# Two Strassen–Winograd products moved to the pre-MLP norm, and the sums of the down weights moved into down

## The chip, the core and the metric

The kernel runs on one core of one Trainium2 chip. The engines that matter here are TensorE (PE, matrix products), VectorE (DVE) and ScalarE (ACT), which work element by element, GpSimd (POOL), and SyncE (SP), on whose queue every transfer of this part of the kernel is issued. Each engine takes its instructions strictly in order; an instruction that waits holds up everything behind it on that engine. The metric is the device time of one execution in microseconds (us), as the median of several runs.

## The reference

One layer of a hybrid decoder trunk, 1024 tokens by 1024 channels, all in float32: two mixers on a common projection, merged and projected, then an MLP with a squared ReLU.

```python
x = x + rms_norm(merged @ w_o, norm_mix_post)
h = rms_norm(x, norm_mlp_pre)
u = jnp.square(jax.nn.relu(h @ w_mlp_up))            # 1024 x 1024 by 1024 x 4096
x = x + rms_norm(u @ w_mlp_down, norm_mlp_post)      # 1024 x 4096 by 4096 x 1024
```

Only the stretch from the last norm on is touched; the mixers ahead of it stay as they are.

## The kernel before, in words

**Precision.** Every float32 operand is split into a high and a low part (h and l at the end of a name: ACT's CAST at L234 makes the high part, DVE's subtraction at L164 the low one), and `mm3` (L254) makes a product of three matmuls: high by high, high by low, low by high. The row of a program order shows the first two as "x2", since they use the same weights.

**Strassen–Winograd.** Both large products of the MLP are made by blocks, two by two, with seven products P1 to P7 in place of eight. In up, the blocks of h are R11, R21, R22 (P1, P2, P3) and four sums, T1 to T4 (P5, P6, P7, P4), called "big" in the trace. The blocks of the weights are made per unit.

**The norm (up to L1130).** Tokens are worked in two halves, u = 0 and 1. For each, PE multiplies by w_o, then four tiles of 128 tokens are normed one by one: x loaded, added, stored (d_x1), squared, scaled (the tile m), transposed by PE in two groups into the banks "t" and "l" (`mt` and `ml` in the trace), and copied and split into the blocks. After the first half R11 and R21 are complete; R22 and T1 to T4 need the second.

**Up (L1133 to L1263)** runs over 16 units n; unit n holds hidden columns 128n on and 2048 + 128n on. `prep(n)` loads the two halves of its weights (wu, 512 KB each) two units ahead, and DVE makes the weight sums P3, P5, P6, P7 of them (four operations). `product` splits one such block of weights (wh, wl: three buffers) and issues 12 matmuls, four steps of three. P1, P6, P7 and P4 add up in one accumulator bank A ("r" for even units, "o" for odd ones, so mr and mo in the trace); after each, the bank is copied out (c11, c12, c22, c21). P2 has a bank of its own, and P5 and P3 share another, C ("g"). The copies, with C added where it belongs, then Relu and Square, give the four blocks of u; `u_sums` (four DVE operations) makes the three sums and one difference that down needs. All seven are stored in d_u. The order by which PE takes a unit's products is written out by hand in the loop: P6, P5, P7, P1 of the next unit, P4, P2 of the next unit, P3.

`down_sums(j)`, in the same loop, loads one row block of the down weights (wd, two loads of 512 KB), makes their four Strassen sums on DVE and stores them (d_t, 1024 KB).

**Down (L1268 to L1366)** makes the seven products again, each over eight steps j; a step is `fetch` (ru from d_u, rv from the weights or from d_t, 512 KB each, four buffers each; both split) and 24 matmuls into four banks of 128 tokens by 512 columns. The order is P1, P2, P6, P5, P7, P4, P3.

**What sets the order.** The Tile framework gives each instruction a priority from its place in the code; `tc.high_priority` moves pieces ahead (HP = 2000 for splits and weight sums, HPM = 1500 for what frees a bank). All transfers go to SP's queue, in the order that comes of this. A tile of a new stage waits until the tile that held its memory before is no longer used.

Of the kernel before, what the change touches and what calls it, by code (L numbers as in the profile page):

```python
# [16 lines left out]
P = 128  # L17
# [114 lines left out]
def kernel(  # L132
# [925 lines left out]
    with tc.tile_pool(name="op", bufs=1, reuse_waits="tile") as op:  # L1058
# [10 lines left out]
        for u in range(2):  # L1069
# [19 lines left out]
            for i in range(4):  # L1089
                t = u * 4 + i  # L1090
                tsl = slice(t * P, t * P + P)
                rs = op.tile([P, 1], F32, tag="rs", name="rs", bufs=3)
                tt(rs, s2s[i][:, 0:1], s2s[i][:, 1:2], ALU.add, eng=G)
                rsqrt(rs, rs, 1.0 / D, EPS)
                m = ms[i]
                xt = op.tile([P, D], F32, tag="xt", name="xt", bufs=2)
                SP.dma_start(out=xt, in_=x2[tsl, :])
                stt(xt, m, rs, xt, ALU.mult, ALU.add)
                SP.dma_start(out=d_x1[tsl, :], in_=xt)
                rs = op.tile([P, 1], F32, tag="rs", name="rs", bufs=3)  # L1100
                act(m, xt, AF.Square, accum_out=rs)
                rsqrt(rs, rs, 1.0 / D, EPS)
                stt(m, xt, rs, wpre2, ALU.mult, ALU.mult)
                il = slice(i * P, i * P + P)
                pv = []
                for g in range(2):
                    pt = mbank("tl"[g])
                    for k in range(4):
                        T.transpose(out=pt[:, k * P:(k + 1) * P], in_=m[:, (g * 4 + k) * P:(g * 4 + k + 1) * P],
                                    identity=ident)  # L1110
                    pv.append(pt.rearrange("p (k c) -> p k c", c=P))
                if u == 0:
                    for g, n in enumerate(("11", "21")):
                        A.copy(out=X[n][:, :, il], in_=pv[g])
                        hilo(R[n], k4, il, X[n][:, :, il])
                else:
                    x11, x21, x12, x22 = (X[n][:, :, il] for n in ("11", "21", "12", "22"))
                    A.copy(out=x12, in_=pv[0])
                    tt(x22, pv[1], x12, ALU.subtract)
                    hilo(R["22"], k4, il, pv[1])  # L1120
                    tt(x12, x12, x11, ALU.subtract)
                    tt(x11, x22, x11, ALU.add)
                    hilo(T2, k4, il, x11)
                    hilo(T1, k4, il, x12)
# [9 lines left out]
    with tc.tile_pool(name="ml", bufs=1, reuse_waits="tile") as ml:  # L1134
# [20 lines left out]
                mm3(ps, hi[:, k, :], lo[:, k, :], RT[p][:, k, :], RT[p][:, 4 + k, :], first and k == 0, k == 3, not first)  # L1155

        def ev(nm):
            return ml.tile([P, 512], F32, tag="ev", name=nm, bufs=8)
# [5 lines left out]
        def store(b, n, t):  # L1164
            SP.dma_start(out=d_u[b, :, n, :], in_=t)


        def down_sums(j):
            w = ml.tile([P, 4, 512], F32, tag="wd", name="wd", bufs=2)
            for f in range(2):  # L1170
                SP.dma_start(out=w[:, 2 * f:2 * f + 2, :].rearrange("p c n -> p (c n)"), in_=wdn[:, j + NU * f, :])
            tt(w[:, 3], w[:, 3], w[:, 1], ALU.subtract)
            tt(w[:, 1], w[:, 1], w[:, 0], ALU.subtract)
            tt(w[:, 0], w[:, 3], w[:, 0], ALU.add)
            tt(w[:, 2], w[:, 2], w[:, 0], ALU.subtract)
            SP.dma_start(out=d_t[:, j], in_=w)

        def s_P1(n):
            x = un[n]
# [14 lines left out]

        def s_P6(n):
            x = un[n]
            product(n, "P6", x["A"], False)
            x["c12"] = ev("c12")
            with tc.high_priority(offset=HPM):
                A.copy(out=x["c12"], in_=x["A"])  # L1200

        def s_P5(n):
            x = un[n]
# [3 lines left out]
        def s_P7(n):  # L1207
            x = un[n]
            product(n, "P7", x["A"], False)
            x["c22"] = ev("c22")  # L1210
            with tc.high_priority(offset=HPM):
                A.copy(out=x["c22"], in_=x["A"])
                tt(x["c22"], x["C"], x["c22"], ALU.add)
            relu2(x["c22"], x["c22"])
            store(2, n, x["c22"])

        def s_P4(n):
# [1 line left out]
            product(n, "P4", x["A"], False)  # L1219
            x["c21"] = ev("c21")  # L1220
            with tc.high_priority(offset=HPM):
                act(x["c21"], x["A"], AF.Relu)
            act(x["c21"], x["c21"], AF.Square)
            store(1, n, x["c21"])

# [40 lines left out]


    with tc.tile_pool(name="dn", bufs=1, reuse_waits="tile") as dn:  # L1268
        wpost2 = dn.tile([P, D], F32, name="wpost2")
        SP.dma_start(out=wpost2, in_=norm_mlp_post[0].unsqueeze(0).broadcast_to([P, D]))  # L1270
        act(wpost2, wpost2, AF.Copy, scale=D ** 0.5)
        sums = dn.tile([P, P], F32, name="sums")[:, 0:3 * NTOK].rearrange("p (t c) -> p t c", c=3)

        def wd_raw(f, c):
            return lambda j: wdn[:, f * NU + j:f * NU + j + 2, c * 512:c * 512 + 512]

        def wd_sum(b):
            return lambda j: d_t[:, j:j + 2, b, :]

        LR = dict(P1=(0, wd_raw(0, 0)), P2=(1, wd_raw(1, 0)), P3=(6, wd_raw(1, 1)), P4=(2, wd_sum(2)),  # L1280
                  P5=(3, wd_sum(1)), P6=(4, wd_sum(0)), P7=(5, wd_sum(3)))

        def fetch(p, j):
            out = []
            for src, tag in ((d_u[LR[p][0], :, j:j + 2, :], "u"), (LR[p][1](j), "v")):
                raw = dn.tile([P, 2, 512], F32, tag="r" + tag, name="r" + tag, bufs=4)
                SP.dma_start(out=raw, in_=src)
                out.append(split(raw, [P, 2, 512], dn, tag, 3))
            return out

        def products(p, banks, first, tail=False):
            todo = []
# [104 lines left out]
```

## Time and profile before

| | before |
|---|---|
| median of 3 runs | 1748.56 us (1748.1 to 1748.99) |
| profiled execution | 1746.59 us |
| its span on the core | 1744.9 us |
| mean granted PE clock | 0.982 |
| PE busy | 1658.3 us (95%) |
| DVE / ACT / POOL busy | 980.7 / 781.5 / 130.7 us |
| HBM read / written | 173.21 / 70.28 MB |

The span is the core's own stretch from first to last instruction; the execution's time is 1.7 us longer. In a "windows" row the stretch and its length stand first, then the busy time of PE, of its weight loads, of DVE, ACT and POOL, each with the number of instructions, then the granted PE clock, the mean busy share of the 16 DMA engines, and GB/s. In a "timeline" row the start and the duration of an instruction stand first, and in brackets at its end the time for which its engine had been idle, and what it waited for. In a row on DMA issues the last figure is the median time from issue to landing.

### The profile page before, as it was taken

To read this page: it belongs to the slowest core of one execution; us is meant where nothing else is said; L and a number is where in the kernel's file an instruction comes from. 1 tells how busy PE (TensorE), PEld (TensorE's weight loads), DVE (VectorE), ACT (ScalarE), POOL (GpSimd) and SP (SyncE) were. 2 spreads that over 40 slices of the span, in tenths; PEclk is the share of its full clock that TensorE was granted. 3 is DMA by queue.
4 is the path that set the end of the run, shared out by engine and by line. 5 is a ranking of instruction groups with operands and counts; after the bars stand their busy time and mean duration, and the time that the engine had idled before them with its cause. 6 is when DMAs were issued, how large, how long until landed. Compare 5 with 4: busy or idle time off the path is not lost.

```text
span 1744.9 us, 24420 instructions
## 1 busy us (share of the span) xinstructions
PE 1658.3 (95%) x9174; PEld 1405.2 (81%) x9174; DVE 980.7 (56%) x1678; ACT 781.5 (45%) x1593; POOL 130.7 (7%) x221
## 2 busy tenths in 40 slices
PE   7999999999999999999999996799999969999997
PEld 6887778878899998998788874588888858888886
DVE  5677466752544436442453466787785544544554
ACT  5455545653433235433321353555555544443442
POOL 2010111111000000101000022000000000000021
PEclk9999999999999999999999997899999989999999
DMA  5222213222212121116543452689884367666663
GB/s 166 58 76 70 80 41 92 78 73 80 61 43 61 44 61 37 50 49 206 162 142 99 139 175 85 222 321 330 318 286 166 122 240 253 194 194 194 194 218 136
DMA packets 168613, 245.10 MB, mean 140 GB/s; under 512 B 21943, under 2 KB 98830, under 8 KB 166446
## 3 DMA queue, kind: packets, MB, share of 16 engines
q1 hardware_dynamic: 168494, 243.53, 42.9%
q8 instruction: 72, 1.18, 0.3%
q14 instruction: 47, 0.39, 0.1%
HBM read 173.21 MB, written 70.28 MB: 140 GB/s over the span
## 4 chain that ended last, share of the span: by engine, by line
PE 81%; DVE 7%; ACT 5%; DMA 4%; issue 2%; POOL 1%; SPq 0%; DVEq 0%; ACTq 0%; POOLq 0%
PE g L66 56%; PE mr L66 9%; PE mo L66 8%; PE ml L66 3%; PE mt L66 3%; DMA gb<-d_g 1%; DVE Xt L164 1%; PE mt L70 1%; DVE Xi L545 1%; DMA oraw<-d_ob 1%; DMA d_sig<-sg 1%; DVE X L164 1%; ACT E L176 1%; DVE wl L164 1%; ACT wh L234 0%
## 5 line engine op out<-in xcount | busy, mean ns | idle before, releaser
L164 DVE TENSOR_TENSOR wl<-w,wh 128x512 fp32r<-128x512 f32 x165 | 114.7, 696 | 224.6 <-ACT wh L234 223.2
L66 PE MATMUL g<-hT,wh 128*128 128x512 f32 (+1 forms) x600 | 239.0, 399 | 1.6 <-DVE gr L173 0.9
L66 PE MATMUL g<-hL,wh 128*128 128x512 f32 (+1 forms) x600 | 232.8, 388 | 0.0
L66 PE MATMUL g<-hT,wl 128*128 128x512 f32 (+1 forms) x600 | 232.0, 387 | 0.0
L234 ACT CAST wh<-w 128x512 fp32r<-128x512 f32 x168 | 104.0, 619 | 203.7 <-PE g L66 179.2
L66 PE MATMUL g<-wh,hT 128*128 128x256 f32 x640 | 185.6, 290 | 0.0
L66 PE MATMUL g<-wl,hT 128*128 128x256 f32 x640 | 182.1, 285 | 0.0
L66 PE MATMUL g<-wh,hL 128*128 128x256 f32 x640 | 182.0, 284 | 0.0
L164 DVE TENSOR_TENSOR ul<-ru,uh 128x1024 fp32r<-128x1024 f32 x56 | 68.6, 1224 | 152.5 <-ACT uh L234 152.2
L66 PEld LDWEIGHTS g<-hT,wh 128*128 128x128 f32 x600 | 113.4, 189 | 22.0 <-ACT sg L176 1.4
L66 PEld LDWEIGHTS g<-hT,wl 128*128 128x128 f32 x600 | 113.3, 189 | 21.5 <-DVE wl L164 0.2
L234 ACT CAST uh<-ru 128x1024 fp32r<-128x1024 f32 x56 | 58.9, 1052 | 159.1 <-PE g L66 92.2
L66 PEld LDWEIGHTS g<-hL,wh 128*128 128x128 f32 x600 | 113.6, 189 | 18.8 <-issue 1.0
L66 PEld LDWEIGHTS g<-wh,hT 128*128 128x128 f32 x640 | 123.1, 192 | 1.4 <-issue 1.0
L66 PEld LDWEIGHTS g<-wl,hT 128*128 128x128 f32 x640 | 123.2, 192 | 1.2 <-issue 1.0
L66 PEld LDWEIGHTS g<-wh,hL 128*128 128x128 f32 x640 | 123.2, 193 | 0.1
L66 PE MATMUL g<-vh,uh 128*128 128x512 f32 x256 | 100.5, 393 | 14.8 <-ACT vh L234 14.8
L66 PE MATMUL g<-vl,uh 128*128 128x512 f32 x256 | 100.5, 393 | 0.0
L66 PE MATMUL g<-vh,ul 128*128 128x512 f32 x256 | 100.3, 392 | 0.0
L176 ACT ACTIVATE c<-c 128x512 f32<-128x512 f32 x112 | 70.7, 632 | 46.9 <-DVE c L164 45.0
L66 PE MATMUL g<-wh,big 128*128 128x512 f32 x256 | 80.5, 392 | 0.0
L66 PE MATMUL g<-R,wh 128*128 128x512 f32 x256 | 78.9, 389 | 0.0
(431 smaller groups left out, 3673.3 us busy)
## 6 DMA issues: line engine op xcount, KB each, us to landing
ru<-d_u SPq DMA_DIRECT2D x56, 512.0 KB, 3.6
w<-in_w_in_dram SPq DMA_DIRECT2D x80, 256.0 KB, 2.7
wu<-in_w_mlp_up_dram SPq DMA_DIRECT2D x32, 512.0 KB, 5.3
wd<-in_w_mlp_down_dram SPq DMA_DIRECT2D x32, 512.0 KB, 5.5
d_u<-c SPq DMA_DIRECT2D x64, 256.0 KB, 2.5
d_t<-wd SPq DMA_DIRECT2D x16, 1024.0 KB, 6.1
rv<-d_t SPq DMA_DIRECT2D x32, 512.0 KB, 4.4
d_u<-us SPq DMA_DIRECT2D x48, 256.0 KB, 2.5
```

The costliest lines, as they stand in the source:

```text
L66: return self.eng.matmul(out, lhsT, rhs, start=start, stop=stop, skip_group_check=more)
L70: return self.eng.transpose(out=out, in_=in_, identity=identity)
L164: (eng or V).tensor_tensor(out=out, in0=a, in1=b, op=op)
L176: A.activation(out=out, in_=a, func=func, **kw)
L234: A.copy(out=hi, in_=raw)
L545: V.tensor_reduce(out=X[:, :, i:i + 1], in_=tv, axis=AX.X, op=ALU.add)
```

## The change

The change has four parts.

1. **P1 and P2 of units 0 to 7 (NE = 8)** are made in the norm, after the code of its second half, in pairs of units: each loads its quarter of the up weights (256 KB), splits it, and multiplies by R11 or R21 into the unit's bank A. P1's bank is copied to a tile e and stored in a new array d_p; P2 is added to it in the bank, goes through Relu and Square, and is stored as block 0 of d_u.
2. **In up**, these units start with P6 in a fresh bank and load P1's result and block 0 again (p1, c11, 256 KB each); where the bank was copied out by ACT, `from_A` adds p1 on DVE. The code's order for them is P6, P5, P7, P3, P4; in PE's queue half of P4 comes ahead of P3. Units 8 to 15 keep all seven products, with the former order. `down_sums` is gone. The tiles "ev" become ten.
3. **Sums of the down weights** are made in down's own `fetch`. P1's also loads two further blocks (rx, ry), takes their difference and stores it as t0; P6 loads t0, adds it to its block and stores t1; P5 loads a second block and subtracts; P4 loads t1 and subtracts; P7 loads t0. The split tiles of both operands become one tile s4 with three buffers, the raw tiles get two buffers each.
4. **Memory**: the blocks are allocated in the order 22, 11, 21, and down's first tiles c12 and c22 come first in its pool, so that they lie over R22, and the first loads and splits over R11 and R21. The load of wpost2 moves behind P1.

```diff
+NE = 8
-    R = {n: hp2.tile([P, 8, 512], F32R, name="R" + n) for n in ("11", "21", "22")}
+    R = {n: hp2.tile([P, 8, 512], F32R, name="R" + n) for n in ("22", "11", "21")}
...
+        for n in range(0, NE, 2):
+            pair = range(n, n + 2)
+            bank = {}
+            for p, k0, blk in (("P1", 0, R["11"]), ("P2", 4, R["21"])):
+                for m in pair:
...
+                    SP.dma_start(out=raw, in_=wup[:, k0:k0 + 4, m * P:m * P + P])
+                    hi, lo = split(raw, [P, 4, P], wsp, "w")
+                    if p == "P1":
+                        bank[m] = mbank("ro"[m % 2])
+                    for k in range(4):
+                        mm3(bank[m], hi[:, k, :], lo[:, k, :], blk[:, k, :], blk[:, 4 + k, :],
+                            p == "P1" and k == 0, k == 3, p == "P2")
+                    e = op.tile([P, 512], F32, tag="e", name="e", bufs=3)
+                    with tc.high_priority(offset=HPM):
+                        if p == "P1":
+                            A.copy(out=e, in_=bank[m])
+                        else:
+                            act(e, bank[m], AF.Relu)
+                    if p == "P2":
+                        act(e, e, AF.Square)
+                    SP.dma_start(out=d_p[m] if p == "P1" else d_u[0, :, m, :], in_=e)
...
-        def down_sums(j):
-            w = ml.tile([P, 4, 512], F32, tag="wd", name="wd", bufs=2)
...
-            SP.dma_start(out=d_t[:, j], in_=w)
+        def from_A(n, out):
+            if n < NE:
+                tt(out, un[n]["A"], un[n]["p1"], ALU.add)
+            else:
+                A.copy(out=out, in_=un[n]["A"])
...
         def s_P6(n):
             x = un[n]
-            product(n, "P6", x["A"], False)
+            if n < NE:
+                x["A"] = mbank("ro"[n % 2])
+                x["p1"], x["c11"] = ev("p1"), ev("c11")
+                SP.dma_start(out=x["p1"], in_=d_p[n])
+                SP.dma_start(out=x["c11"], in_=d_u[0, :, n, :])
+            product(n, "P6", x["A"], n < NE)
...
         for n in range(2):
             prep(n)
-            s_P1(n)
-            s_P2(n)
         for n in range(NU):
             s_P6(n)
             s_P5(n)
             s_P7(n)
-            if 1 < n + 1 < NU:
+            if NE <= n + 1 < NU:
                 s_P1(n + 1)
-            down_sums(n)
-            s_P4(n)
-            if 1 < n + 1 < NU:
+                s_P4(n)
                 s_P2(n + 1)
-            s_P3(n)
+                s_P3(n)
+            else:
+                s_P3(n)
+                s_P4(n)
...
+        LR = dict(P1=(0, w_(0, 0)), P2=(1, w_(1, 0)), P6=(4, w_(0, 0), t_(0), ALU.add, t_(1)),
+                  P5=(3, w_(0, 1), w_(0, 0), ALU.subtract), P7=(5, t_(0)),
+                  P4=(2, w_(1, 0), t_(1), ALU.subtract), P3=(6, w_(1, 1)))
...
         def fetch(p, j):
...
+            b, src, *more = LR[p]
+            u, v = load("ru", d_u[b, :, j:j + 2, :]), load("rv", src(j))
+            if more:
+                w = load("rx", more[0](j))
+                tt(v, v, w, more[1])
+                for to in more[2:]:
+                    SP.dma_start(out=to(j), in_=v)
...
+            if p == "P1":
+                v, w = load("rx", w_(1, 1)(j)), load("ry", w_(0, 1)(j))
+                tt(v, v, w, ALU.subtract)
+                SP.dma_start(out=t_(0)(j), in_=v)
```

**The norm's second half, on PE.** Before, the eight transposes of the second half (mt and ml of the four tiles m) stand in a row, and P1 of unit 0 (mr from R11) comes behind them:

```order
L70 MATMUL mt_10447<-ident_77,m_10104 128x128 x4
L70 MATMUL ml_10452<-ident_77,m_10104 128x128 x4
L70 MATMUL mt_10481<-ident_77,m_10106 128x128 x4
L70 MATMUL ml_10486<-ident_77,m_10106 128x128 x4
L70 MATMUL mt_10515<-ident_77,m_10108 128x128 x4
L70 MATMUL ml_10520<-ident_77,m_10108 128x128 x4
L70 MATMUL mt_10549<-ident_77,m_10110 128x128 x4
L70 MATMUL ml_10554<-ident_77,m_10110 128x128 x4
L66 MATMUL mr_10592<-R11_9646,wh_10593 128x512 x2
```

In the changed kernel the transposes of the first tile m stand in the middle of P1 of unit 1 (mo from R11), with P2 of unit 0 (mr from R21) to follow:

```order
L67 MATMUL mo_10599<-R11_9648,wl_10596 128x512
L67 MATMUL mo_10599<-R11_9648,wh_10595 128x512 x2
L71 MATMUL mt_10448<-ident_77,m_10105 128x128 x4
L71 MATMUL ml_10453<-ident_77,m_10105 128x128 x4
L67 MATMUL mo_10599<-R11_9648,wl_10596 128x512
L67 MATMUL mo_10599<-R11_9648,wh_10595 128x512 x2
L67 MATMUL mo_10599<-R11_9648,wl_10596 128x512
L67 MATMUL mr_10577<-R21_9649,wh_10617 128x512 x2
```

So the transposes moved from ahead of the first product to fixed places among the sixteen.

**The same place, on SP's queue.** The loads of unit 0's weights (wu) stood behind the stores of x (d_x1); now they stand behind the stores of the last tiles e:

```order
L1151 DMA d_p_95<-e_10854 128x512
L1151 DMA d_p_95<-e_10876 128x512
L1151 DMA d_u_93<-e_10897 128x512
L1151 DMA d_u_93<-e_10919 128x512
L1168 DMA wu_10937<-in_w_mlp_up_dram 128x8x128 x2
L1168 DMA wu_10945<-in_w_mlp_up_dram 128x8x128 x2
L1221 DMA p1_10954<-d_p_95 128x512
L1222 DMA c11_10955<-d_u_93 128x512
```

Each e comes from PE's bank by way of ACT, and the two of d_u are of units 6 and 7, the last products in the norm.

**Up, around unit 5, on PE.** Before, P1 of the next unit stood between P7 (from big) and P4 (from the next big) of a unit; the first row of each product is shown:

```order
L66 MATMUL mo_11023<-big_10570,wh_11164 128x512 x2
...
L66 MATMUL mr_11186<-R11_9646,wh_11187 128x512 x2
...
L66 MATMUL mo_11023<-big_10571,wh_11213 128x512 x2
...
L66 MATMUL g_11233<-R21_9647,wh_11234 128x512 x2
...
L66 MATMUL g_11147<-R22_9648,wh_11254 128x512 x2
```

Now, behind the last step of P7 (mr from the first big) stand the first two matmuls of P6 of the next unit (mo), and then half of P4, and P3 (g), of this one:

```order
L67 MATMUL mr_11437<-big_10923,wh_11477 128x512 x2
L67 MATMUL mr_11437<-big_10923,wl_11478 128x512
L67 MATMUL mo_11558<-big_10433,wh_11563 128x512 x2
L67 MATMUL mr_11437<-big_10924,wh_11518 128x512 x2
L67 MATMUL mr_11437<-big_10924,wl_11519 128x512
...
L67 MATMUL g_11460<-R22_9647,wh_11499 128x512 x2
```

The products between P7 and P4 went to the norm, and the first step of the next P6 took their place.

**Up, the same unit, on DVE in the changed kernel.** From the sum of c12 with C (g, complete with P3) to the sum of p1 with bank A for the next unit's c12:

```order
L165 TENSOR_TENSOR c12_11458<-g_11460,c12_11458 128x512
L165 TENSOR_TENSOR ss_11553<-ss_11553,wu_11550 128x512
L165 TENSOR_TENSOR wu_11550<-wu_11550 128x512
L165 TENSOR_TENSOR ss_11553<-wu_11550,ss_11553 128x512
L165 TENSOR_TENSOR wl_11583<-ss_11432,wh_11582 128x512
L165 TENSOR_TENSOR wl_11599<-wu_11429,wh_11598 128x512
L165 TENSOR_TENSOR c21_11534<-mr_11437,p1_11438 128x512
L165 TENSOR_TENSOR wl_11621<-ss_11432,wh_11620 128x512
L165 TENSOR_TENSOR us_11539<-c12_11458,c22_11493 128x512
L165 TENSOR_TENSOR us_11540<-us_11539,c11_11439 128x512
L165 TENSOR_TENSOR c12_11579<-mo_11558,p1_11559 128x512
```

That copy of bank A for c12 stood on ACT before (L1200); it now is the eleventh row on DVE.

**From up to down, on SP's queue.** Before, behind the last store of the last unit's sums (us):

```order
L1165 DMA d_u_93<-us_13183 128x512
L1270 DMA wpost2_13198<-in_norm_mlp_post_dram 128x1024
L1287 DMA ru_13222<-d_u_93 128x1024
L1287 DMA rv_13228<-in_w_mlp_down_dram 128x2x512
L1287 DMA ru_13258<-d_u_93 128x1024
L1287 DMA rv_13264<-in_w_mlp_down_dram 128x2x512
```

In the changed kernel, behind the same store:

```order
L1191 DMA d_u_93<-us_13136 128x512
L1316 DMA ru_13163<-d_u_93 128x1024
L1316 DMA rv_13165<-in_w_mlp_down_dram 128x2x512
L1316 DMA rx_13172<-in_w_mlp_down_dram 128x2x512
L1316 DMA ry_13174<-in_w_mlp_down_dram 128x2x512
L1316 DMA ru_13202<-d_u_93 128x1024
L1316 DMA rv_13204<-in_w_mlp_down_dram 128x2x512
L1335 DMA d_t_94<-rx_13172 128x1024
L1316 DMA rx_13211<-in_w_mlp_down_dram 128x2x512
```

The first ru still stands behind the last store of up; a step of P1 now has four loads and a store in place of two loads.

More of the change, by code (lines that the diff above doesn't have):

```diff
@@ L1157, in ev @@
         def ev(nm):
[L1158 removed]
+            return ml.tile([P, 512], F32, tag="ev", name=nm, bufs=10)
         def relu2(r, src):
@@ L1165, in store @@
             SP.dma_start(out=d_u[b, :, n, :], in_=t)
-        def down_sums(j):
-            w = ml.tile([P, 4, 512], F32, tag="wd", name="wd", bufs=2)
[L1170 to L1175, printed above, removed]
-            SP.dma_start(out=d_t[:, j], in_=w)
+        def from_A(n, out):
[3 more added lines that the diff above has]
+                A.copy(out=out, in_=un[n]["A"])
         def s_P1(n):
@@ L1196, in s_P6 @@
             x = un[n]
-            product(n, "P6", x["A"], False)
+            if n < NE:
[4 more added lines that the diff above has]
+            product(n, "P6", x["A"], n < NE)
             x["c12"] = ev("c12")
             with tc.high_priority(offset=HPM):
-                A.copy(out=x["c12"], in_=x["A"])
+                from_A(n, x["c12"])
         def s_P5(n):
@@ L1211, in s_P7 @@
             with tc.high_priority(offset=HPM):
-                A.copy(out=x["c22"], in_=x["A"])
+                from_A(n, x["c22"])
                 tt(x["c22"], x["C"], x["c22"], ALU.add)
@@ L1221, in s_P4 @@
             with tc.high_priority(offset=HPM):
-                act(x["c21"], x["A"], AF.Relu)
+                if n < NE:
+                    from_A(n, x["c21"])
+                    act(x["c21"], x["c21"], AF.Relu)
+                else:
+                    act(x["c21"], x["A"], AF.Relu)
             act(x["c21"], x["c21"], AF.Square)
@@ L1268 @@
     with tc.tile_pool(name="dn", bufs=1, reuse_waits="tile") as dn:
[L1269 to L1274, printed above, removed]
-            return lambda j: wdn[:, f * NU + j:f * NU + j + 2, c * 512:c * 512 + 512]
-        def wd_sum(b):
-            return lambda j: d_t[:, j:j + 2, b, :]
@@ L1280, with keep @@
-        LR = dict(P1=(0, wd_raw(0, 0)), P2=(1, wd_raw(1, 0)), P3=(6, wd_raw(1, 1)), P4=(2, wd_sum(2)),
-                  P5=(3, wd_sum(1)), P6=(4, wd_sum(0)), P7=(5, wd_sum(3)))
-        def fetch(p, j):
[L1284 to L1289, printed above, removed]
+        def keep(nm):
+            return [dn.tile([P, 512], F32, name=f"{nm}{i}") for i in range(4)]
@@ new lines, with w_, t_, load @@
+        c12, c22 = keep("c12"), keep("c22")
+        def w_(f, c):
+            return lambda j: wdn[:, f * NU + j:f * NU + j + 2, c * 512:c * 512 + 512]
+        def t_(b):
+            return lambda j: d_t[b, :, j:j + 2, :]
+        LR = dict(P1=(0, w_(0, 0)), P2=(1, w_(1, 0)), P6=(4, w_(0, 0), t_(0), ALU.add, t_(1)),
+                  P5=(3, w_(0, 1), w_(0, 0), ALU.subtract), P7=(5, t_(0)),
+                  P4=(2, w_(1, 0), t_(1), ALU.subtract), P3=(6, w_(1, 1)))
+        def load(tag, src):
+            raw = dn.tile([P, 2, 512], F32, tag=tag, name=tag, bufs=2)
+            SP.dma_start(out=raw, in_=src)
+            return raw
@@ new lines, in fetch @@
+        def fetch(p, j):
+            b, src, *more = LR[p]
[5 more added lines that the diff above has]
+                    SP.dma_start(out=to(j), in_=v)
+            s4 = dn.tile([P, 4, 2, 512], F32R, tag="s4", name="s4", bufs=3)
+            with tc.high_priority(offset=HP):
+                for i, raw in ((0, u), (2, v)):
+                    A.copy(out=s4[:, i], in_=raw)
+                    tt(s4[:, i + 1], raw, s4[:, i].bitcast(F32), ALU.subtract)
+            if p == "P1":
+                v, w = load("rx", w_(1, 1)(j)), load("ry", w_(0, 1)(j))
+                tt(v, v, w, ALU.subtract)
+                SP.dma_start(out=t_(0)(j), in_=v)
+            return (s4[:, 0], s4[:, 1]), (s4[:, 2], s4[:, 3])
@@ L1309, in plain @@
                 pass
-        def keep(nm):
-            return [dn.tile([P, 512], F32, name=f"{nm}{i}") for i in range(4)]
-        c11, c12, c22, c21 = (keep(nm) for nm in ("c11", "c12", "c22", "c21"))
         def half(src, t, c):
@@ L1335 @@
         plain("P1", Ab, True)
+        c11, c21 = keep("c11"), keep("c21")
+        wpost2 = dn.tile([P, D], F32, name="wpost2")
+        SP.dma_start(out=wpost2, in_=norm_mlp_post[0].unsqueeze(0).broadcast_to([P, D]))
+        act(wpost2, wpost2, AF.Copy, scale=D ** 0.5)
+        sums = dn.tile([P, P], F32, name="sums")[:, 0:3 * NTOK].rearrange("p (t c) -> p t c", c=3)
         for i in range(4):
```

6 lines of the change are left out of this document (5 added, 1 removed).

## The prediction

> **What bounds the kernel now.** I read the page's span and chain, then the waits of the matmul engine from 1060 us on, then busy time by stretches, then the timeline at each gap.
>
> ```profile
> span 1744.9 us, 24420 instructions
> PE 81%; DVE 7%; ACT 5%; DMA 4%; issue 2%; POOL 1%; SPq 0%; DVEq 0%; ACTq 0%; POOLq 0%
> ...
> PE mt L70 <- DVE m L173: 16.0, 4, 5.9
> PE g L66 <- ACT vh L234: 14.8, 1, 14.8
> PE mr L66 <- ACT wh L234: 12.4, 1, 12.4
> ...
> 1066.00:1104.00 38.00, 8.69 (x36) 6.39 (x34) 33.74 (x44) 19.53 (x35) 10.44 (x18) 0.56 0.32 112
> 1104.00:1412.00 308.00, 306.84 (x1343) 253.19 (x1344) 221.06 (x347) 166.08 (x285) 0.00 (x0) 0.99 0.71 252
> 1412.00:1427.00 15.00, 0.47 (x3) 0.04 (x1) 4.40 (x6) 4.23 (x5) 0.00 (x0) 0.60 0.74 247
> 1427.00:1440.00 13.00, 12.73 (x45) 9.86 (x46) 8.58 (x8) 6.38 (x7) 0.00 (x0) 0.81 1.04 412
> 1440.00:1735.00 295.00, 294.66 (x1300) 243.64 (x1299) 145.41 (x140) 121.98 (x148) 13.76 (x12) 1.00 0.61 198
> ```
>
> The matmul engine (PE, first column after the length) carries the end: full in up (1104 to 1412) and down (1427 to 1735), idle in the norm and for 15 us between up and down. These gaps are what can be won; what can be lost is that either full stretch stops being full. In down the transfers move 198 GB/s; in the burst after 1427, with many waiting, 412 GB/s at a share of 1.04, which I take as the ceiling.
>
> The pace: four steps of three matmuls make one product of 12.
>
> ```profile
> 1399.77 0.62 PE L66 MATMUL mo<-big,wh 128*128 128x512 f32 x2
> 1400.45 0.62 PE L66 MATMUL g<-big,wh 128*128 128x512 f32 x2
> ```
>
> 0.68 us a step, so a product is 2.72 us, and a step of j in down (24 matmuls) 5.44 us.
>
> **Norm: 19 us won.**
>
> ```profile
> 1066.19 0.39 PE L66 MATMUL g<-wh,big 128*128 128x512 f32 x1
> 1021.12 0.63 PE L70 MATMUL mt<-ident,m 128*128 128x128 f32 x4 [0.50 <-DVE m L173]
> 1021.59 0.60 PE L70 MATMUL ml<-ident,m 128*128 128x128 f32 x4
> 1098.90 4.35 SPq L1142 DMA_DIRECT2D wu<-in_w_mlp_up_dram  x4
> 1103.24 1.14 ACT L234 CAST wh<-wu 128x512 fp32r<-128x512 f32 x2 [2.46 <-DMA wu<-in_w_mlp_up_dram]
> 1103.91 1.22 PE L66 MATMUL mr<-R,wh 128*128 128x512 f32 x2 [12.41 <-ACT wh L234]
> 1106.39 0.62 ACT L234 CAST wh<-wu 128x512 fp32r<-128x512 f32 x1 [2.01 <-DMA wu<-in_w_mlp_up_dram]
> ```
>
> Before, PE is free of w_o at 1066.6 (call it N) and starts the first product 37.3 us later. Now 16 products stand in that gap: 16 x 2.72 = 43.5 us. The eight transposes add 3.8 at a warm clock (0.47 from mt to ml). They stand in PE's queue behind fixed counts of matmuls, while their m comes from ACT, POOL and DVE, whose queues now also hold casts and evacuations: I walk the four tiles in the order shown and find PE waiting 1.4, 1.4, 1.0 and 0.9 us, so N+52. Then a new wait: up's first weights (wu) stand in SP's queue behind the store of the last e, whose Relu and Square end 1.5 us after P2(7), so they are issued at N+54. P6(0) needs both halves of unit 0: before, the first of four such loads landed 4.3 us after 1098.90 and the third 7.5 us after, so the second about 5.9 us after; two ss sums (0.69 each), the cast (0.62): P6(0) at N+62. Won: 37.3 + 43.5 - 62 = 18.8 us. The clock is cold at the first product on both sides.
>
> **Up, units 0 to 7: 12 us lost.** The five products of a unit take 13.6 us. DVE has 18 operations there (five wl, four of prep, three sums with p1, two with C, four of us); before it had 22, down's sums among them, in 19 us.
>
> ```profile
> 1124.67 0.39 PE L66 MATMUL mr<-big,wl 128*128 128x512 f32 x1
> 1124.87 0.62 ACT L234 CAST wh<-ss 128x512 fp32r<-128x512 f32 x1 [2.10 <-PE mr L66]
> 1125.54 0.74 PE L66 MATMUL mo<-big,wh 128*128 128x512 f32 x2 [0.48 <-ACT wh L234]
> ...
> 1129.19 0.69 DVE L164 TENSOR_TENSOR wu<-wu 128x512 f32<-128x512 f32 x1
> 1129.79 0.68 DVE L164 TENSOR_TENSOR ss<-wu,ss 128x512 f32<-128x512 f32 x1
> 1130.39 0.69 DVE L164 TENSOR_TENSOR wl<-ss,wh 128x512 fp32r<-128x512 f32 x1
> ```
>
> Two matmuls of P6(n+1) now follow P7(n) in PE's queue, as they did before in unit 0 alone; their weights take P7's buffer, so the cast starts only when P7 is nearly through. There PE was free at 1124.90 and went on at 1125.54: 0.64, for seven units 4.5 us. The second wait: P7(n) overwrites bank A, so it waits until DVE has added p1 for c12, and this is the eleventh operation behind c12's sum with P3(n-1). At 0.60 us apart (0.72 where one needs the one ahead) the eleventh ends about 7.2 us after P3, while PE needs 6.35 us (half of P4, ten matmuls of P6, P5): 0.8 in five units, nothing in units 0 and 2, and 2.1 in unit 3, where P4's wl stands ahead of the sum and waits for P5. That is 6, and 1.5 more where wu lands late (its second half is issued behind a unit's last sums). What is queued behind each such sum is the next unit's wl, so the delay is not made up. Bounds: 0, if DVE never falls behind, to 17. I take 12. Dropping down's 64 sums and 32 MB of traffic from up gains nothing, since PE was full beside them.
>
> **Up to down: 4.5 us won, not 14.8.**
>
> ```profile
> 1412.08 0.39 PE L66 MATMUL g<-R,wl 128*128 128x512 f32 x1
> 1417.20 0.32 SPq L1165 DMA_DIRECT2D d_u<-us  x1
> 1417.61 0.40 SPq L1270 DMA_DIRECT2D wpost<-in_norm_mlp_post_dram  x1
> 1418.11 0.40 SPq L1287 DMA_DIRECT2D ru<-d_u  x1
> 1424.80 1.04 ACT L234 CAST uh<-ru 128x1024 fp32r<-128x1024 f32 x1 [0.20 <-DMA ru<-d_u]
> 1427.21 1.22 DVE L164 TENSOR_TENSOR vl<-rv,vh 128x1024 fp32r<-128x1024 f32 x1
> 1427.23 1.22 PE L66 MATMUL g<-vh,uh 128*128 128x512 f32 x2 [14.76 <-ACT vh L234]
> ```
>
> The new addresses would allow loads 20 us earlier, since ru and rv now lie over R11, but SP's order keeps the first ru behind the last store of u_sums(15). That store comes sooner: P4 is last now and needs only Relu, Square and one sum, and P3 is through 1.8 us earlier, so ru is issued about 3.2 us after the last product (T) instead of 5.6, with no wpost2 (512 KB) ahead. ru lands at T+7.8 and the first product starts at T+10.2 instead of T+14.8. Bounds: 2 to 7.
>
> **Down, P1: 13 us lost.** Per j it now moves ru, rv, rx, ry and the store of t0, 5 x 512 KB = 2.62 MB, in 5.44 us of PE: 482 GB/s, above the 412 seen at a share of 1.04. At 412 one transfer takes 1.27 us and five 6.36. SP is also in order: the store of j+1 waits for DVE's subtraction, which waits for rx and ry, issued behind the store of j.
>
> ```profile
> ru<-d_u SPq DMA_DIRECT2D x56, 512.0 KB, 3.6
> ...
> d_u<-c SPq DMA_DIRECT2D x64, 256.0 KB, 2.5
> ...
> rv<-in_w_mlp_down_dram SPq DMA_DIRECT2D x24, 512.0 KB, 5.7
> ```
>
> A 256 KB store lands 2.5 us after its issue, 0.64 of it data, so 1.9 are fixed. A turn is three transfers (3.8), 1.9, DVE's 1.22 and 0.3 of semaphores and issue: 7.2 us. The first store goes at T+13, the eighth at T+63.5; rv of P2's first j stands behind it, lands at T+68 and is cast at T+69.3. Without the limit P2 would start at T+56 (10.2, eight times 5.44, 2.4 of cold clock as before). Bounds: 7 (turns of 6.36) to 21 (turns of 8.35, below). By the Trainium skill, page "DMA: Bandwidth & Descriptors", section "Where 436 GB/s comes from", transfers between HBM and SBUF are bound at about 358 GB/s; the burst of 412 above speaks against it here, and by it five transfers would take 7.3 us and this term would be about 20.
>
> **Down, the rest: 2 us lost.** P6 moves four transfers, 5.1 of 5.44 us, with rv two steps on waiting for a store to complete; I take 2, bounds 0 and 8. P5 and P4 move three (3.8), the others two. DVE's extra 1.22 us per j and the shallower buffers lie under 5.44 us of PE. The tail is as before.
>
> **The sum**: -18.8 + 12 - 4.5 + 13 + 2 = +3.7 us on the profiled execution's 1746.59, so 1750.3. The median of the runs is 1748.56, 2 above that execution; on its level the forecast is **1752**, slower by 0.2%, which is about what a measurement of this kernel can tell from no change.
>
> **Rivals.**
> *DVE keeps ahead in up* (the other side). If DVE's eleven operations take under 6.3 us, by 0.52 apart instead of 0.60, or ACT's cast comes early, P7 never waits; the 12 us go and the time is 1740. For it: DVE was busy 221 of 308 us before with more work. Against: its order, and the 0.60. 22%.
> *Mixed traffic is slower than the burst of loads.*
>
> ```profile
> 1150.00:1200.00 50.00, 50.00 (x222) 41.44 (x221) 39.53 (x62) 27.94 (x48) 0.00 (x0) 1.00 0.90 317
> ```
>
> With stores among them transfers moved 317 GB/s at a share of 0.90, 352 when full: five take 7.45 us and, with 0.9 of gap, a turn 8.35. P1 then loses 21 and the time is 1760. Against it: part of that mix were small packets. 23%.
> *The clock falls in P1.* PE would be busy 5.44 of 7.2 us, with pauses of 1.8. At half clock 24 matmuls take 10.9 us, and P1's eight steps some 30 us longer than at 7.2: about 1780. Against it: the clock stayed full through pauses of up to 2 us elsewhere. 4%. The Trainium skill, page "TensorE: Matmul & The Clock Gate", section "HAM oscillation — how this bites in real kernels", lets the clock fall when waits for DMA pass a window of about 3.4 us; by it these pauses are too short, though the one ahead of P2 may not be.
> *The change does what its words say*: loads prefetched into up, P1 fed from them. The order speaks against it; it would give another 10 us in the gap, 1742. 6%.
>
> **Numbers.** The forecast 45%: half of it within 0.2% of 1748.56 (1745.1 to 1752.1), half above. Rival one and the last are faster, the second and third slower. Faster 0.27, same 0.25, slower 0.48. Range 1738 to 1766: it takes in the first two rivals' own times and the bounds of the gap and of P6, and leaves out the clock and sums of several bad ends.
>
> **What would show it.** Norm: P1 and P2 run through with four short waits on m, then about 10 us of PE idle on wu. Up: units 0 to 7 of about 15.2 us each, PE waiting on DVE c12 and ACT wh. Gap: about 10 us. P1: a DMA share at 1.0 and steps of 7 us. Wrong it would be if units take 13.6, if wu is loaded before the last e, or if P1's steps take under 6.3.

## The result, and the profile after

The changed kernel takes 1765.41 us (median of 4 runs, 1763.17 to 1767.85), the kernel before 1748.33 on the same chips: a ratio of 1.0099 (95% interval 1.0082 to 1.0117), slower by 1.0%. The forecast was 1752, slower by 0.2%, with 1738 to 1766 as its range. The profiled execution took 1766.43 us against 1746.59, 19.8 more, with a span of 1764.7.

The stages are cut at the same events in both kernels. Of before, only the start of P2 in down is still wanted (timeline):

```profile
1473.38 0.39 PE L66 MATMUL mt<-vh,uh 128*128 128x512 f32 x1
```

In the timeline of the changed kernel these rows are the last matmul with w_o, the last of the sixteen products moved into the norm, SP's loads of up's first weights (wu), up's first product, up's last matmul, and the first of down's P1 and P2:

```profile
1067.00 0.39 PE L67 MATMUL g<-wh,big 128*128 128x512 f32 x1
1117.66 0.39 PE L67 MATMUL mo<-R,wl 128*128 128x512 f32 x1
1119.81 4.48 SPq L1168 DMA_DIRECT2D wu<-in_w_mlp_up_dram  x4
1127.89 1.22 PE L67 MATMUL mr<-big,wh 128*128 128x512 f32 x2 [9.84 <-ACT wh L236]
1406.36 0.39 PE L67 MATMUL mo<-big,wl 128*128 128x512 f32 x1
1417.72 2.91 PE L67 MATMUL g<-s 128*128 128x512 f32 x5 [10.97 <-ACT s L1330]
1488.92 0.80 PE L67 MATMUL mt<-s 128*128 128x512 f32 x1 [5.92 <-ACT s L1330]
```

| stage | before | after | change | forecast |
|---|---|---|---|---|
| to the last matmul with w_o | 1066.6 | 1067.4 | +0.8 | 0 |
| from there to up's first product (16 products, 43.5 us, moved in) | 37.3 | 60.5 | +23.2 - 43.5 = -20.3 | -18.8 |
| up's first product to its last matmul (the 43.5 moved out) | 308.6 | 278.9 | -29.7 + 43.5 = +13.8 | +12 |
| up's end to down's first product | 14.8 | 11.0 | -3.8 | -4.5 |
| down's P1 | 46.2 | 71.2 | +25.0 | +13 |
| P2 to the end of the span | 271.5 | 275.8 | +4.3 | +2 |
| sum | | | +19.8 | +3.7 |

Every term that was forecast as a change has the sign that was forecast, and all but one are within 2.3 us. P1 is 12 us over its term, and over its bound of 21. In windows of the changed kernel (up's units 0 to 7, the rest of up, the gap, P1, the rest of down) it is the one long stretch where PE is not full, 54 of 71 us, at a DMA share of 0.89 and 301 GB/s:

```profile
1127.90:1250.00 122.10, 113.23 (x466) 88.78 (x467) 85.62 (x139) 49.14 (x82) 0.00 (x0) 0.97 0.57 184
1250.00:1406.80 156.80, 156.07 (x688) 128.57 (x686) 92.42 (x143) 86.64 (x147) 0.00 (x0) 1.00 0.41 144
1406.80:1417.70 10.90, 0.00 (x0) 0.00 (x0) 3.82 (x6) 3.39 (x5) 0.00 (x0) 0.59 0.84 297
1417.70:1488.90 71.20, 54.17 (x192) 39.58 (x192) 29.30 (x24) 19.83 (x21) 0.00 (x0) 0.88 0.89 301
1488.90:1752.00 263.10, 262.07 (x1142) 215.88 (x1143) 161.91 (x152) 110.32 (x133) 12.40 (x10) 0.99 0.80 274
```

One turn of P1 in the timeline, without PE: from one store of t0 (d_t) to the next.

```profile
1428.59 0.34 SPq L1335 DMA_DIRECT2D d_t<-rx  x1
1429.02 0.39 SPq L1316 DMA_DIRECT2D rx<-in_w_mlp_down_dram  x1
1429.45 0.83 SPq L1316 DMA_DIRECT2D ry<-in_w_mlp_down_dram  x1
1430.33 0.55 SPq L1316 DMA_DIRECT2D ru<-d_u  x1
1430.99 0.38 SPq L1316 DMA_DIRECT2D rv<-in_w_mlp_down_dram  x1
...
1435.30 1.23 DVE L165 TENSOR_TENSOR rx<-rx,ry 128x1024 f32<-128x1024 f32 x1 [2.25 <-DMA ry<-in_w_mlp_down_dram]
1436.56 0.34 SPq L1335 DMA_DIRECT2D d_t<-rx  x1
```

SP issues the store and four loads, and then stands for 5.2 us until ry has landed and DVE has subtracted: 6.7 us from the store to the subtraction, 1.26 from there to the next store, 8.0 in all. The eight stores go from 1420.51 to 1482.46, 8.85 us apart on average, with turns from 7.8 to 10.4. PE needs 5.44. It is the circle that the forecast described, but slower. In the longest turn (1436.56 to 1446.97) the DMA engines run out of work while SP waits (the last two numbers are their busy share and GB/s):

```profile
1445.00:1446.50 1.50, 0.17 (x1) 0.00 (x0) 0.79 (x1) 0.00 (x0) 0.00 (x0) 1.00 0.22 85
```

### The profile page after: what moved, and what is told of

It reads as the page before. It is cut to its first block, busy times and chain, and to the rows that moved or that the text cites. A ratio compares the mean times of both kernels' runs of the same rounds, so it can differ in the third digit from the quotient of the medians.

```text
span 1764.7 us, 24397 instructions
## 1 busy us (share of the span) xinstructions
PE 1672.0 (95%) x9174; PEld 1406.1 (80%) x9174; DVE 988.4 (56%) x1662; ACT 773.9 (44%) x1577; POOL 131.5 (7%) x221
## 5 line engine op out<-in xcount | busy, mean ns | idle before, releaser
L165 DVE TENSOR_TENSOR wl<-w,wh 128x512 fp32r<-128x512 f32 x181 | 125.8, 695 | 228.5 <-ACT wh L236 226.3
L236 ACT CAST wh<-w 128x512 fp32r<-128x512 f32 x184 | 113.9, 619 | 211.5 <-PE g L67 188.2
L67 PE MATMUL g<-s 128*128 128x512 f32 x768 | 185.1, 402 | 22.1 <-ACT s L1330 21.8
L67 PEld LDWEIGHTS g<-s 128*128 128x128 f32 x768 | 147.7, 194 | 59.1 <-ACT s L1330 24.8
L1330 ACT CAST s<-ru 128x1024 fp32r<-128x1024 f32 x56 | 58.8, 1050 | 134.8 <-PE mo L67 42.0
L165 DVE TENSOR_TENSOR s<-ru,s 128x1024 fp32r<-128x1024 f32 x56 | 68.5, 1223 | 75.4 <-ACT s L1330 75.1
L1330 ACT CAST s<-rv 128x1024 fp32r<-128x1024 f32 x56 | 58.8, 1049 | 54.5 <-DVE rv L165 44.8
L177 ACT ACTIVATE c<-c 128x512 f32<-128x512 f32 x104 | 65.2, 631 | 35.0 <-DVE c L165 33.5
L165 DVE TENSOR_TENSOR s<-rv,s 128x1024 fp32r<-128x1024 f32 x56 | 68.4, 1222 | 20.7 <-ACT s L1330 20.6
```

Source lines behind the costliest of these rows:

```text
L67: return self.eng.matmul(out, lhsT, rhs, start=start, stop=stop, skip_group_check=more)
L165: (eng or V).tensor_tensor(out=out, in0=a, in1=b, op=op)
L177: A.activation(out=out, in_=a, func=func, **kw)
L236: A.copy(out=hi, in_=raw)
L1330: A.copy(out=s4[:, i], in_=raw)
```

## The experiments

The ratios are to runs of the kernel before on the same chip (medians 1746.6 to 1747.4 us). The questions in order: which part loses, what sets P1's turn, what up's and the norm's waits are worth, and what is left when they are taken away.

### Down alone

```diff
-NE = 8
+NE = 0
...
         for n in range(2):
             prep(n)
+            s_P1(n)
+            s_P2(n)
...
-            if NE <= n + 1 < NU:
+            if 1 < n + 1 < NU:
```

> P1 and P2 of all units are back in up, in the order of before (without the down sums); memory, down and the sums of down weights as in the changed kernel. Theory: down costs what the trace shows there, +25 us in P1 and +4 behind it, and the shorter gap between up and down gives 4 back; taking the down sums out of up gives nothing, since PE was full beside them: 1748.3 + 25 = about 1773 (1770 to 1776), slower than the changed kernel. Rival: the loss of the change sits in up's waits, and down is cheap: 1750 to 1755. Second rival: up gets faster without the down sums: under 1768.

1769.43 us, ratio 1.0126 (1.0109 to 1.0143), 0.6 us below the expected range. Windows for up, gap, P1 and the rest:

```profile
1105.20:1414.10 308.90, 307.74 (x1344) 253.63 (x1344) 183.43 (x284) 167.77 (x285) 0.00 (x0) 0.99 0.42 143
1414.10:1425.20 11.10, 0.03 (x1) 0.00 (x0) 3.83 (x6) 3.48 (x5) 0.00 (x0) 0.64 0.85 286
1425.20:1495.70 70.50, 53.00 (x192) 39.10 (x192) 29.25 (x25) 19.93 (x21) 0.00 (x0) 0.89 0.89 304
1495.70:1758.00 262.30, 261.27 (x1142) 215.30 (x1143) 162.09 (x152) 110.26 (x133) 12.40 (x10) 0.99 0.80 275
```

Up takes 308.9 us, as before the change (308.6), though 64 sums are gone from DVE and traffic has fallen from 252 to 143 GB/s: dropping them is worth nothing under a full PE. Down costs the same as in the full change, 70.5 us in P1. The whole loss is down's. The moved products are worth the difference of the two ratios, some 0.27% or 4.7 us; the two intervals overlap, so this is a rough figure (-20.3 + 13.8 = -6.5 by the stages).

### P1 without t0, and without its store

The first leaves out rx, ry, subtraction and store in P1, the second the store alone; in both, P6 and P7 read another weight block in place of t0.

```diff
-            if p == "P1":
-                v, w = load("rx", w_(1, 1)(j)), load("ry", w_(0, 1)(j))
-                tt(v, v, w, ALU.subtract)
-                SP.dma_start(out=t_(0)(j), in_=v)
...
-        LR = dict(P1=(0, w_(0, 0)), P2=(1, w_(1, 0)), P6=(4, w_(0, 0), t_(0), ALU.add, t_(1)),
-                  P5=(3, w_(0, 1), w_(0, 0), ALU.subtract), P7=(5, t_(0)),
+        LR = dict(P1=(0, w_(0, 0)), P2=(1, w_(1, 0)), P6=(4, w_(0, 0), w_(1, 1), ALU.add, t_(1)),
+                  P5=(3, w_(0, 1), w_(0, 0), ALU.subtract), P7=(5, w_(1, 1)),
```

> The changed kernel without t0: P1 loads only its two operands, and P6 and P7 read the weight block (1,1) where they read t0, so a part of down's product is left out; transfers and operations of P6 and P7 are as many as before. Theory: the whole loss of P1 comes with rx, ry and the store, so its steps fall from 8.85 to 5.44 us, 25 us less: 1740 (1738 to 1743). Rival: two raw buffers in place of four and the shared split tiles slow P1 as well: 1748 or more.

> The changed kernel, but the difference t0 is not stored, and P6 and P7 read the weight block (1,1) where they read t0, so a part of down's product is left out; rx, ry and the subtraction stay in every step of P1. Theory (bytes under PE's time: four loads are 2.1 MB, 5.1 us at 412 GB/s or 6.1 at 345): P1 loses 0 to 6 us, 1738 to 1744. Rival (the wait of the queue on DVE is the price, not the bytes; the queue still waits for the buffers that DVE frees): steps of 7 us or more, 1750 or more.

1737.69 us, ratio 0.9947 (0.9931 to 0.9962), and 1743.91, ratio 0.9985 (0.9976 to 0.9994). P1 in windows, first without t0, then without the store:

```profile
1416.00:1461.90 45.90, 45.86 (x192) 37.41 (x193) 22.61 (x19) 20.92 (x22) 0.00 (x0) 0.95 0.89 302
```

```profile
1417.30:1465.90 48.60, 46.31 (x192) 37.34 (x192) 29.29 (x25) 19.74 (x22) 0.00 (x0) 0.95 0.92 359
```

Without t0, P1 is back at 45.9 us: fewer buffers and shared split tiles cost nothing there. Four loads and the subtraction, without the store, cost 2.7 us more in P1. So the price comes with the fifth transfer, or with the circle that it closes.

### The store one step later, with two buffers and with three

```diff
-                v, w = load("rx", w_(1, 1)(j)), load("ry", w_(0, 1)(j))
-                tt(v, v, w, ALU.subtract)
-                SP.dma_start(out=t_(0)(j), in_=v)
+                late.append((j, load("rx", w_(1, 1)(j)), load("ry", w_(0, 1)(j))))
+            while len(late) > (p == "P1"):
+                i, v, w = late.pop(0)
+                tt(v, v, w, ALU.subtract)
+                SP.dma_start(out=t_(0)(i), in_=v)
```

> The changed kernel, but rx and ry of a step are subtracted and stored one step later, behind the next step's loads; bytes and operations are the same. Theory (round trip: the queue stands while ry lands and DVE subtracts, and only then issues the next loads): steps fall from 8.85 to the time of five transfers at 412 GB/s, 6.4 us, so P1 loses 8 us and not 25: 1748 (1745 to 1752). Rival (the rate with stores among the loads is the bound, 315 to 350 GB/s): steps of 7.5 to 8.3 us, 1755 to 1761. No change at all would mean that neither is it.

1758.48 us, ratio 1.0061 (1.0044 to 1.0078): what the rate theory wanted. Stores stand 7.9 us apart. But it was no clean test, by what SP's queue waited for between 1420 and 1480 us (us in total, times, longest):

```profile
SPq L1316 <- DMA d_t<-rx: 29.0, 6, 6.2
```

With two buffers, the next load into rx waits until the store that reads this buffer, the one issued just ahead, has landed, and all loads behind it in the queue wait with it. Hence three:

```diff
-            raw = dn.tile([P, 2, 512], F32, tag=tag, name=tag, bufs=2)
+            raw = dn.tile([P, 2, 512], F32, tag=tag, name=tag, bufs=2 + (tag in ("rx", "ry")))
```

> As e3, with three buffers in place of two for rx and ry, so that no load of P1 waits for the subtraction just ahead of it. Theory (rate: with a store among them and all five shared by the same engines, 345 GB/s are moved when full, 7.6 us for 2.62 MB): steps of 7.6 to 8 us as in e3, 1754 to 1759. Rival (round trip: e3 still had it, through the two buffers): steps of 6.4 us at 412 GB/s, 1745 to 1750.

1747.37 us, ratio 1.0000 (0.9990 to 1.0009). The rate theory, expected to give 1754 or more, falls. SP's rows of a turn, and a window over P1's steps:

```profile
1438.83 0.34 SPq L1339 DMA_DIRECT2D d_t<-rx  x1
1439.27 0.38 SPq L1316 DMA_DIRECT2D ru<-d_u  x1
1439.74 0.89 SPq L1316 DMA_DIRECT2D rv<-in_w_mlp_down_dram  x1
1440.68 0.55 SPq L1316 DMA_DIRECT2D rx<-in_w_mlp_down_dram  x1
1441.28 0.52 SPq L1316 DMA_DIRECT2D ry<-in_w_mlp_down_dram  x1
1445.20 0.34 SPq L1339 DMA_DIRECT2D d_t<-rx  x1
```

```profile
1419.00:1465.00 46.00, 43.89 (x178) 32.97 (x178) 25.85 (x22) 15.30 (x15) 0.00 (x0) 0.98 1.04 410
```

The turn shown is 6.37 us (6.42 on average over seven): five transfers of 512 KB at 412 GB/s, 1.27 each, with nothing added. The same bytes, with the same stores among them, that moved at 301 GB/s in the change move at 410. P1 takes 53.9 us (1416.47 to 1470.38), 7.8 more than before, near the forecast's lower bound of 7. The Trainium skill, page "DMA: Bandwidth & Descriptors", section "Where 436 GB/s comes from", binds transfers between HBM and SBUF at about 358 GB/s; this row does not agree, 410 for 46 us.

### t0 in every other step of P1 and P2

```diff
-            if p == "P1":
+            if (p, j // 2 % 2) in (("P1", 0), ("P2", 1)):
                 v, w = load("rx", w_(1, 1)(j)), load("ry", w_(0, 1)(j))
```

> The changed kernel, but t0 is made in every other step of P1 and P2 in place of every step of P1; bytes and operations in all are the same. Theory (P1 loses because five transfers a step do not fit under 5.44 us of PE; four and three a pair of steps do at the 345 GB/s that DMA engines moved when full there, 3.67 MB in 10.6 of 10.9 us): of P1's 25 us, 18 to 25 come back, 1740 to 1747. Rival (what costs is the round trip of the store, DVE and the next loads in one queue, and it costs wherever it stands): half of the steps, but the same eight round trips, so 1755 or more.

1749.48 us, ratio 1.0020 (1.0010 to 1.0029), between the two expectations. P1 takes 47.0 us, and P2 is full too:

```profile
1415.60:1462.60 47.00, 46.17 (x193) 37.27 (x193) 24.37 (x21) 19.27 (x21) 0.00 (x0) 0.95 0.93 333
1462.60:1506.80 44.20, 44.10 (x192) 35.87 (x192) 26.70 (x24) 18.02 (x22) 0.00 (x0) 1.00 0.95 336
```

All eight circles are still there, but one of some 8 us now has two steps, 10.9 us of PE, to run in. Of 24 us won in P1, a new wait of 4.8 gives a part back at P6's start, where the addition of t0 stands behind P2's sums on DVE.

### Bank A copied by ACT

```diff
-                tt(out, un[n]["A"], un[n]["p1"], ALU.add)
+                A.copy(out=out, in_=un[n]["A"])
+                tt(out, out, un[n]["p1"], ALU.add)
```

> The changed kernel, but for units 0 to 7 bank A is copied out by ACT, as before the change, and DVE adds p1 to the copy; one ACT operation more for each of three copies a unit. Theory: PE's waits for DVE's c (5.4 us in six pieces) go, and with the pause of 1.96 us in unit 3 the stretch of half clock behind it (2.3 us): 1757.5 (1756 to 1760). Rival: DVE as a whole is late (86 of 122 us busy and in order), the waits come back as waits for wl or C: 1763 to 1766.

1754.41 us, ratio 1.0047 (1.0033 to 1.0062). Waits of PE in units 0 to 7, in the change and then here (us in total, times, longest):

```profile
PE mo L67 <- DVE c L165: 3.3, 3, 2.0
PE mr L67 <- DVE c L165: 2.1, 3, 0.8
PE mo L67 <- ACT wh L236: 2.0, 4, 0.5
PE mr L67 <- ACT wh L236: 1.4, 3, 0.5
```

```profile
PE mo L67 <- ACT wh L236: 2.0, 4, 0.5
PE mr L67 <- ACT wh L236: 1.4, 3, 0.5
PE g L67 <- DVE c L165: 0.4, 1, 0.4
```

The 5.4 us of waits for c are gone but for 0.4, and up is 7.8 us shorter (1126.76 to 1397.82). The rest of the 11 stands in P1 (66.9 us against 71.2), whose code is the same: its turns differ from one execution to the next.

### The norm's and up's ends: SP's order

In the first, ml's other tiles are allocated ahead of wu, so that wu lies over m, and wu's first loads get a higher priority; in both, the stores that stand ahead of the next stage's loads are issued by ACT.

```diff
+            if n == 0:
+                ev("ev"), ml.tile([P, 512], F32, tag="us", name="us", bufs=4)
             raw = ml.tile([P, 2, 8, P], F32, tag="wu", name="wu", bufs=2)
...
-                SP.dma_start(out=raw[:, f], in_=wup[:, :, c0:c0 + P])
+                with tc.high_priority(offset=2500 if n < 2 else 0):
+                    SP.dma_start(out=raw[:, f], in_=wup[:, :, c0:c0 + P])
...
-                    SP.dma_start(out=d_p[m] if p == "P1" else d_u[0, :, m, :], in_=e)
+                    (A if n == NE - 2 else SP).dma_start(out=d_p[m] if p == "P1" else d_u[0, :, m, :], in_=e)
```

> The changed kernel, but the tiles wu lie over those of m (free when the last transposes are done), and the stores of the last two units' e in the norm are issued by ACT, so that up's first weight loads no longer stand behind them in SP's queue. Theory (the 9.8 us ahead of up's first product are SP's order, not memory or DMA rate): wu is issued about 9 us sooner, PE goes on with no pause and a warm clock: 9 to 12 us less, 1754 to 1757. Rival (the loads are slow there because stores and casts crowd the queues, or ACT gets late by its four DMA issues): under 4 us, 1762 or more.

```diff
-            SP.dma_start(out=d_u[b, :, n, :], in_=t)
+            (A if n == NU - 1 else SP).dma_start(out=d_u[b, :, n, :], in_=t)
```

> The changed kernel, but the last unit's stores are issued by ACT, so that down's first loads stand behind the stores of unit 14 in SP's queue. Theory (the 11 us between up and down are the loads' time behind SP's order; the memory under them is free): the loads land inside up, and only the casts, behind the last stores on ACT, are left, T+5 to T+6 in place of T+11: 5 to 6 us less in the gap, up to 1758 to 1761. Rival: P1 is bound by transfers, so the earlier start is given back there: 1764 to 1766.

1752.10 us, ratio 1.0033 (1.0021 to 1.0045), and 1756.86, ratio 1.0061 (1.0046 to 1.0076). The timeline of the first, then of the second:

```profile
1110.72 2.54 SPq L1175 DMA_DIRECT2D wu<-in_w_mlp_up_dram  x3
1120.86 1.17 PE L67 MATMUL mr<-big,wh 128*128 128x512 f32 x2 [2.37 <-ACT wh L236]
```

```profile
1399.58 0.32 SPq L1316 DMA_DIRECT2D ru<-d_u  x1
1412.76 1.22 PE L67 MATMUL g<-s 128*128 128x512 f32 x2 [5.43 <-ACT s L1330]
```

wu is issued 9.1 us sooner (1110.72 against 1119.81), and the pause ahead of up falls from 9.84 to 2.37; ru goes inside up, and the pause ahead of down falls from 10.97 to 5.43. Ahead of down, the pause was SP's order: only the issuer of the stores changed. The memory laid over R11 was free, as the change meant it to be; the first ru and rv did not go, because the stores ahead of them in the queue had not. Ahead of up, SP's order held wu too: in the changed kernel the last store of e is issued at 1119.37 and wu 0.44 us behind it, with no wait of its own. Whether the old place in memory would also have held wu is not shown, since this edit moved the memory and the order at once. P1 took 66.8 and 68.4 us here, so 4.4 and 2.8 of the two gains are not the edits'.

### All together

> The changed kernel with four edits together: copies of bank A by ACT, t0 in every other step of P1 and P2, wu over m with e stored by ACT, and the last unit's stores by ACT. Theory: the gains add up, 11 (measured alone) + 20 + 10 + 5 = 46 us from 1765: 1719 (1715 to 1726), faster than the kernel before. Rival: they share one limit, transfers in down, and half is given back: 1735 to 1745.

1731.39 us, ratio 0.9915 (0.9900 to 0.9930): faster than both kernels, 0.85% below the one before. The four single gains (11.0, 15.9, 13.3, 8.6) make 48.8; taking off the 11.5 that three of them owe to P1's turns (4.3, 4.4, 2.8), 37.3 are left, and 34.0 came, between the two expectations. By the ratios to before on the same chips the four gains are smaller, 41 us, or some 30 without P1's part, and together they made 32: the gains add up as far as these differences can tell. Two further steps were tried on top of it: four weight buffers in up and the addition of t0 at high priority on DVE; then that addition without the four buffers, with the last unit's stores issued by POOL.

```diff
-            hi, lo = split(un[n][p], [P, 4, P], wsp, "w")
+            hi, lo = split(un[n][p], [P, 4, P], ml, "w", 4)
...
-                tt(v, v, w, more[1])
+                with tc.high_priority(offset=HP):
+                    tt(v, v, w, more[1])
```

> e8 with two more edits: the addition of t0 in down goes ahead of the sums of P2 on DVE (it stood behind them, PE idle 4.8 us at P6's start and 1.95 later), and up's split weights have four buffers of their own (PE waited 0.48 us in each of seven units for the cast into the third). Theory: 6 to 9 us from the first, with half clock behind those pauses, and 3 from the second: 1731 - 10 = 1721 (1718 to 1726). Rival: the waits move on to the next late operation: 1727 to 1732.

```diff
-            (A if n == NU - 1 else SP).dma_start(out=d_u[b, :, n, :], in_=t)
+            (G if n == NU - 1 else SP).dma_start(out=d_u[b, :, n, :], in_=t)
```

> e8, with the last unit's stores issued by POOL in place of ACT, so that down's first casts no longer stand behind them, and with the addition of t0 ahead of the sums of P2 on DVE, as in e11 (without its four weight buffers). Theory: the pause between up and down falls from 5.4 to about 3 us, and that at P6's start by 2 to 4: 1731 - 5 = 1726 (1722 to 1729). Rival: the second step's split tile lies over the tiles that are being stored, and POOL's transfers end later than ACT's, so what the first step wins the second one waits: 1729 to 1733.

1732.21 us, ratio 0.9916 (0.9902 to 0.9930), and 1733.97, ratio 0.9921 (0.9907 to 0.9934): the three are not told apart, and both times are the rival's, or beside it. In the first, the wait at P6's start falls from 4.80 to 2.99 us and the seven waits for wh inside up are gone, but four waits for c, 3.9 us in all, stand in their place (two are shown first below); in the second, down starts after 3.33 us instead of 5.42, and its second step waits:

```profile
1135.73 0.80 PE L67 MATMUL g<-R,wh 128*128 128x512 f32 x1 [2.26 <-DVE c L165]
1164.07 0.74 PE L67 MATMUL g<-R,wh 128*128 128x512 f32 x2 [1.34 <-DVE c L165]
```

```profile
1391.99 0.79 PE L67 MATMUL g<-s 128*128 128x512 f32 x1 [3.33 <-ACT s L1335]
1404.77 1.08 PE L67 MATMUL g<-s 128*128 128x512 f32 x2 [3.63 <-ACT s L1335]
```

## Why the prediction was right, and where it was not

The time, 1765.41, lies 13 us above the forecast and 0.6 us inside the end of its range. The direction came by the mechanism that was described, but that the range held owes something to luck: the sum's own term for P1 was far too small, and the range reached so far up only for a rival and for other terms' bounds.

- **The bound** held: PE's pauses in the norm and between the stages were what could be won, full PE hid the rest, and dropping the down sums from up gave nothing (e1).
- **The norm** held: 20.3 won against 18.8. The four waits on m are 2.7 us in all (4.7 forecast), then PE stands 9.84 us for wu, "about 10" in the forecast. That wu stood behind the stores of e in SP's queue is in the trace, and e6, which changed order and memory together, took 7.5 us of the wait away.
- **Up** held, 13.8 against 12, by the two waits that were named: 5.4 us for c (6 forecast, with 1.96 in unit 3 where 2.1 was worked out) and 3.4 for the cast (4.5). The rival that DVE keeps ahead falls. What was missed is the clock; with about 1.9 us for it these make 10.7 of the 13.8, and the other 3 were not placed. "The clock stayed full through pauses of up to 2 us elsewhere" was wrong on the trace of before itself, where half clock follows a pause of 1.89 us (at 127 us); here it follows the pause in unit 3:

```profile
1182.67 0.70 PE L67 MATMUL mo<-big,wh 128*128 128x512 f32 x2 [1.96 <-DVE c L165]
```

  The windows behind it have the granted clock as the third number from the end, down to 0.50:

```profile
1182.00:1184.00 2.00, 1.32 (x5) 1.13 (x6) 1.73 (x3) 0.00 (x0) 0.00 (x0) 0.88 0.76 291
1184.00:1186.00 2.00, 2.00 (x6) 1.52 (x6) 0.00 (x0) 0.00 (x0) 0.00 (x0) 0.50 0.88 282
1186.00:1188.00 2.00, 1.56 (x5) 0.89 (x4) 0.71 (x2) 0.62 (x1) 0.00 (x0) 0.76 0.93 257
```

  P7 of that unit takes 4.6 us instead of 2.7.
- **The gap** held: 3.8 against 4.5. "Prefetched as its words say" falls, for the reason given, SP's order (e7).
- **P1** is the term that failed in size: 25 against 13. The step was "a turn is three transfers (3.8), 1.9, DVE's 1.22 and 0.3": 7.2 us. DVE's part held (1.26); from the store to the landing of ry the trace shows 6.5 to 9.2 us, 7.6 on average, in place of 5.7. The seven turns are 1.65 us longer each, 11.6 of the 12 missing. The transfers were priced at 412 GB/s, and a DMA share of 1.0 was forecast; 301 GB/s at 0.89 were measured, which is 338 when full, against 394 in e9 (410 at 1.04). So about 1.0 us of a turn is engines without work, and about as much is transfers that were slower while they ran. The rival that came nearest in time, "mixed traffic is slower than the burst of loads" (1760), was near that rate with its 352, but its reason falls: with loads always queued the same mix moves at 410 GB/s (e9). Why the transfers of the circle are slower while they run stays open. The circle, not the bytes, made P1's steps 8 to 9 us; the bytes alone make 6.4 (e9) and PE 5.4 (e2).
- **The clock in P1**: it did fall, four times, but behind the first step it cost little, since the turn and not PE set the pace; it shows after the 5.92 us ahead of P2, within the next term.
- **P6 and behind**: 4.3 against 2, mostly P2's first matmuls at half clock (until 1494.14, so about 2.6 us).

That the median moved by 17.1 and the profiled execution by 19.8 is within P1's own spread: with the same code for it, P1 took 71.2, 70.5, 68.4, 66.9 and 66.8 us in five profiled executions.

## What to carry to other kernels

When a load, an operation on it and a store go round in one in-order queue, price the whole circle, and let the next loads stand in the queue ahead of the store that waits: here one step of lag was worth 7 us with two buffers and 18 with three. A prefetch needs free memory and a free place in the queue; look at what stands ahead of the load before counting on the memory. Work moved into a pause pays its way only as far as the stage that it left can run faster: of 20 us won in the norm, 14 were lost again in up, most of them to waits that a longer unit had covered.

## What the runs showed of the hardware that was not expected

- A pause of PE need not be long for half clock. In the fourteen traces, from 1060 us on, one of the six pauses from 1.33 to 1.77 us was followed by it, and 15 of the 25 from 1.81 to 2.5 us were, for 3.41 us each. The same wait in unit 3 (1.9 to 2.3 us) led to it in five of eight executions. The Trainium skill, page "TensorE: Matmul & The Clock Gate", section "HAM oscillation — how this bites in real kernels", sets the limit at idle gaps above about 3.4 us; these rows do not agree.
- Packets took longer in the circle: in P1 of the change 8% of the packets of 2 KB took over 100 ns (84 is usual), in e9, with the queue kept full and the same bytes, 0.6%. That the queue runs dry each turn is not shown to be the cause. Why single turns took 10 us and others 7.8 was not found.
